# Output projection by block products: where the weights' parts are made, and which queues and engines carry the residual and the results

## The chip, the core and the metric

The kernel runs on one core of one Trainium2 chip. The core has five engines that run side by side, each with its own queue of instructions: TensorE (PE, matrix products into PSUM banks), VectorE (DVE), ScalarE (ACT), GpSimd (POOL) and SyncE (SP, which here only issues transfers). ACT and POOL can issue transfers too. The metric is the device time of one execution in microseconds, the median of several runs, smaller is better.

## The reference

One decoder block on x of shape (1, 2048, 1024), all in float32:

```python
h = rmsnorm(x, attn_norm);  z = h @ w_in          # pool | q | k | v | two gates
a = pool_mixer(...);        b = swa_sink_attention(...)
x = x + (g_pool * a + g_attn * b) @ w_out         # the output projection, w_out 1024 x 1024
h = rmsnorm(x, ffn_norm)
up = causal_depthwise_conv(h @ w_up, conv_w, conv_b)
x = x + (silu(up[..., :2816]) * up[..., 2816:]) @ w_down
```

The change concerns the third line, in the second half of the sequence.

## The kernel before, in words

**Chunks.** The 2048 positions are worked in two chunks of 1024 (`c` = 0, 1). In a chunk follow: keys and values (8 blocks), the attention loop (4 groups of 8 blocks, with projections as "fillers" between), the gates (`gates`, six units in chunk 1), the output projection, the up-projection (22 units) and the down-projection (`Down`).

**Three products for one.** A float32 operand is split into a high part (a cast by ACT) and the rest (a subtraction by DVE); a product is the sum of three matmuls of these parts. A split therefore costs one ACT and one DVE instruction per tile, and the result takes twice the room.

**Block products.** In chunk 1 the output projection uses Strassen's scheme in Winograd's form: w_out and its input are cut into 2 x 2 blocks, and seven products of sums of blocks replace eight. `PRODUCTS` (L198) lists them in order: A11·B11, A12·B21, S2·T2, S3·T3, A22·T4, S1·T1, S4·B22, called products 0 to 6 here. The A's and S's are blocks, or sums and differences of blocks, of w_out; the B's and T's are those of the input, made by `right_first`, `right_t1` to `right_t4` and `right_b22` (a subtraction on DVE and `parted`, a split). A product is 48 matmuls of 128x128 by 128x512 into four PSUM banks (`mul`), 8 steps of 6. The lists of banks `x` and `y` are shared: products 0, 2, 3 and 4 add into `x` one after the other, products 1, 5 and 6 use `y`, so a bank must be read out between two of them.

**Weights.** `out_factors` (L396) is a generator that the mixer of chunk 1 steps along, block by block in the keys' loop and in the attention loop. For each of four pairs of rows of blocks it loads `w_out` twice 512 KB into R tiles, and makes all seven A's and S's with 16 sums and differences in all. Each of the 28 results is split at once (`part`: ACT L406, DVE L407) into another R tile and stored to memory (`wo_A..`, `wo_S..`), both parts. `Out.weights` (L1242) later loads the two ready 1 MB tiles of one product, one product ahead of its use. R is a pool of three tiles (4 KB per partition), shared with the raw weights of the gates and of the up-projection; U is a pool of 19 tiles (8 KB).

**Results.** After product 0 `kept(0, 0)` (L1270) copies four banks, halved, by ACT (L1274) and adds the residual x by two transfers of POOL that accumulate into the tile (L1277); the same happens after products 2 and 3 for the other blocks. `final` (L1283) adds a finished bank to such a tile on DVE (L1285), squares it on ACT (L1289, L1292), adds up the squares for the next norm (DVE L1296), and stores the tile to `x2d` through SP. `residual` loads x plainly by SP instead. `stats` (L1346) sums the squares over channels by small matmuls (L669), takes the power on POOL (L662), and `whole` spreads the result by transposes (L680); `right_first` for the up-projection (L1177, then `parted`) needs that.

**Order.** The function `out_blocks` (L1303) is the text's order. On each engine the build lays out the instructions in one fixed order: text order is a preference, and an instruction whose inputs are expected ready can be put ahead. On the chip each engine then runs strictly in that order, so an instruction that waits holds up everything behind it on its engine. SP issues transfers in such an order too.

Of the kernel before, what the change touches and what calls it, by code (L numbers as in the profile page):

```python
# [26 lines left out]
P = 128  # L27
# [195 lines left out]
def block_kernel(ctx: ExitStack, tc: tile.TileContext, x, xT, pos, vec, qkn, w_poolT, w_pool, w_q, w_kv,  # L223
# [170 lines left out]
    out_parts = {name: dp.tile([P, 4, 2, 4, P], F32, f"wo_{name}") for name, _ in PRODUCTS}  # L394

    def out_factors():  # L396

        one, two = slice(4, 8), slice(0, 4)
        for i in range(4):
            g, v = (rp.tile([P, 8, P], F32, "R") for _ in range(2))  # L400
            load(g, w_out[i])
            load(v, w_out[i + 4])

            def part(name, src, i=i):
                t = rp.tile([P, 2, 4, P], F32R, "R")
                A.copy(t[:, 0], src)  # L406
                V.tensor_sub(t[:, 1], src, t[:, 0].bitcast(F32))  # L407
                load(out_parts[name][:, i], t.bitcast(F32))

            yield  # L410
            part("A11", g[:, one])
            yield
            part("A12", g[:, two])
            yield
            part("A22", v[:, two])
            yield
            V.tensor_sub(v[:, one], g[:, one], v[:, one])
            V.tensor_sub(v[:, two], v[:, two], v[:, one])
            part("S3", v[:, one])
            yield  # L420
            part("S2", v[:, two])
            yield
            V.tensor_add(g[:, one], g[:, one], v[:, two])
            part("S1", g[:, one])
            yield
            V.tensor_sub(g[:, two], g[:, two], v[:, two])
            part("S4", g[:, two])
            yield
# [801 lines left out]
    class Out:  # L1230


        def __init__(self, c):
            self.c, self.m, self.w, self.b, self.xs = c, [], [], {}, {}
            self.accs = [[], []]
# [16 lines left out]
        def mul(self, i, banks, first=False, by_pair=False):  # L1252

            w, r = self.w[i], self.b[PRODUCTS[i][1]]
            for n in range(8):
                j, m = divmod(n, 4) if by_pair else divmod(n, 2)[::-1]
                at = 0
                for k in range(2):
                    for a, b in ((0, 0), (0, 1), (1, 0)):
                        nc.tensor.matmul(banks[m], w[m // 2][:, m % 2, a, (2 * j + k + 2) % 4],  # L1260
                                         r[j][:, b, k], start=(first and j == 0 and at == 0),
                                         stop=(j == 1 and at == 5), skip_group_check=True)
                        at += 1
                yield n
# [5 lines left out]
        def kept(self, h, n, banks):  # L1270

            x = self.xs[h, n] = up_.tile([P, 4, 512], F32, "U")
            for m in range(4):
                A.activation(x[:, m], banks[m], AF.Copy, scale=0.5)  # L1274
            for i in range(2):
                m = slice(2 * i, 2 * i + 2)
                G.dma_start(x[:, m], self.rest(h, n)[:, m], accum_op=ALU.add)  # L1277

# [4 lines left out]
        def final(self, h, n, m, bank):  # L1283
            x = self.xs[h, n][:, m]
            V.scalar_tensor_tensor(x, bank, 0.5, x, op0=ALU.mult, op1=ALU.add)  # L1285
# [11 lines left out]
            load(x2d[4 * h + m][:, n * 512:n * 512 + 512], x)  # L1297
# [5 lines left out]
    def out_blocks(ob):  # L1303
# [19 lines left out]
        run(1, y, True, True)  # L1323
        t2s = right_t2(ob.m, ob.b, None)
# [3 lines left out]
        run(2, x)  # L1328
        right_t3(ob.m, ob.b)
        ob.kept(0, 1, x)  # L1330
        ob.weights()
        run(3, x)
        right_t4(ob.m, ob.b, t2s)
        ob.residual(1, 0)
        ob.kept(1, 1, x)
        ob.weights()
        for n in ob.mul(4, x):
            if n % 2 == 1:
                ob.final(1, 0, n // 2, x[n // 2])
        right_b22(ob.m, ob.b)  # L1340
        ob.weights()
        stream.fetch(stream.used + 1)
        stream.part(stream.used + 1)
# [8 lines left out]
        for n in ob.mul(5, y, True):  # L1352
            if n == 2:
                stats(0)
# [7 lines left out]
        for n in ob.mul(6, y):  # L1362
            if n == 0:
                for j in range(2, 4):
                    right_first(xg, b, j, pb)
# [4 lines left out]
            if n % 2 == 1:  # L1370
                ob.final(0, 1, n // 2, y[n // 2])
# [238 lines left out]
    def gates(c, units, b, xg, last_probabilities, last_values, last_filler):  # L1610


        def weights(f, n):
            if f < len(units):
# [6 lines left out]
                if n and w.at == 4:  # L1621
                    stream.fetch(stream.used + (1 if c > 0 or f + 1 < len(units) else 2))
# [49 lines left out]
        for f in range(2, n):  # L1672
# [9 lines left out]
            if f == n - 1 and c > 0:  # L1682
# [3 lines left out]
                ob.weights()  # L1686
            elif f == n - 1:
                mixes = {j: mixed(j) for j in (3, 2, 1)}
# [386 lines left out]
```

## Time and profile before

| | us |
|---|---|
| Median of 3 runs (2422.41 to 2429.26) | 2424.63 |
| The profiled execution | 2422.86 |
| Its span, first to last instruction | 2421.1 |
| TensorE busy in the span | 2370.1 |
| VectorE busy | 1907.9 |
| ScalarE busy | 1181.4 |
| GpSimd busy | 186.5 |

All breakdowns come from the profiled execution; between its span and its time lie 1.8 us. A row of the timeline gives start and length in us, engine, line, operation, output and input tiles, shape and count, and in brackets how long the engine had been idle and what released it. A row of a group by line gives busy us, mean ns of one, and the idle time ahead of the group with its releasers. "s", "a", "t" and "f" are PSUM tiles. `<-issue` means that the profile shows no other engine or transfer that was waited for. The granted clock is TensorE's, 1.00 at full speed.

### The profile page before, as it was taken

Reading aid. Unit: us, or ns where it says so; the run is one execution under the profiler, and the core shown is the slowest. Engines: PE = TensorE matmul, PEld = TensorE weight load, DVE = VectorE, ACT = ScalarE, POOL = GpSimd, SP = SyncE. Lnnn points to the kernel's source line nnn. Section 1 sums busy time; section 2 is a strip of 40 time slices with the busy share of each in tenths; the row PEclk is TensorE's granted clock in tenths of the full one; section 3 lists DMA queues with packets and bytes.
Section 4 is the critical chain, followed back from the end, with each engine's and each line's share of the span. In section 5 each row is a group of like instructions: output and inputs, shape, how many; then the busy total and the mean of one; then the engine's idle time right before and its main releaser. Section 6 shows DMA issues by size and latency. Waiting matters only on the chain.

```text
span 2421.1 us, 30322 instructions
## 1 busy us (share of the span) xinstructions
PE 2370.1 (98%) x11080; PEld 1962.8 (81%) x11080; DVE 1907.9 (79%) x2948; ACT 1181.4 (49%) x2166; POOL 186.5 (8%) x128
## 2 busy tenths in 40 slices
PE   8999998999999999999999999999999999999999
PEld 8888887877888888788888788778778888888887
DVE  8687887876977777899956878787478777779994
ACT  7455455454555555643533554454336545454432
POOL 1123111000000000000002232200100000000000
PEclk9999999999999999999999999999999999999999
DMA  9767777688222333644354797766842222228411
GB/s 342 245 202 234 226 227 260 211 290 293 80 79 91 101 105 105 213 167 142 125 214 139 231 296 240 234 205 248 286 161 90 90 90 79 79 70 287 139 70 53
DMA packets 167349, 425.94 MB, mean 176 GB/s; under 512 B 14624, under 2 KB 50976, under 8 KB 155680
## 3 DMA queue, kind: packets, MB, share of 16 engines
q1 hardware_dynamic: 160784, 412.28, 49.7%
q0 software_dynamic: 5984, 11.54, 3.0%
q8 instruction: 87, 1.43, 0.2%
q14 instruction: 62, 0.51, 0.1%
q10 hardware_dynamic: 432, 0.19, 0.0%
HBM read 274.66 MB, written 149.29 MB: 175 GB/s over the span
## 4 chain that ended last, share of the span: by engine, by line
PE 47%; DVE 4%; DMA 3%; issue 3%; ACT 1%; POOL 0%; SPq 0%; POOLq 0%; DVEq 0%; ACTq 0%
PE f L1225 11%; PE t L1225 6%; PE f L266 5%; PE f L1846 4%; PE a L1846 4%; PE s L1846 4%; PE t L1846 4%; PE a L1225 3%; PE a L266 1%; DMA U<-xT 1%; DVE F L1030 1%; PE a L974 1%; PE s L1260 1%; DMA tad<-U 1%; PE s L913 1%
## 5 line engine op out<-in xcount | busy, mean ns | idle before, releaser
L266 PE MATMUL f<-U,U 128*128 128x512 f32 (+1 forms) x2496 | 586.6, 390 | 9.6 <-ACT U L249 4.8
L266 PEld LDWEIGHTS f<-U,U 128*128 128x128 f32 x2496 | 457.2, 188 | 105.2 <-DVE U L250 7.3
L1225 PE MATMUL f<-U,U 128*128 128x512 f32 x1872 | 448.1, 390 | 6.9 <-ACT Q L1387 3.4
L1225 PEld LDWEIGHTS f<-U,U 128*128 128x128 f32 x1872 | 351.1, 188 | 83.5 <-ACT Q L1387 5.5
L1435 DVE SCALAR_TENSOR_TENSOR M<-F,vc,M 128x1024 f32<-128x1024 f32 x176 | 225.1, 1281 | 140.8 <-ACT M L1432 140.5
L1225 PE MATMUL t<-U,U 128*128 128x512 f32 x1332 | 316.1, 390 | 0.2 <-ACT Q L1387 0.2
L1225 PEld LDWEIGHTS t<-U,U 128*128 128x128 f32 x1332 | 250.5, 188 | 52.7 <-ACT Q L1387 0.8
L362 ACT CAST U<-R 128x1024 fp32r<-128x1024 f32 x147 | 153.7, 1053 | 87.3 <-DVE R L391 42.8
L1225 PE MATMUL a<-U,U 128*128 128x512 f32 x756 | 184.6, 391 | 0.0
L363 DVE TENSOR_TENSOR U<-R,U 128x1024 fp32r<-128x1024 f32 x147 | 179.2, 1221 | 3.0 <-ACT U L362 3.0
L1225 PEld LDWEIGHTS a<-U,U 128*128 128x128 f32 x756 | 141.3, 188 | 29.3 <-ACT Q L1387 0.2
L1225 PE MATMUL f<-U,M 128*128 128x512 f32 x624 | 151.1, 390 | 0.8 <-DVE F L1413 0.8
L932 ACT ACTIVATE Q<-s,st,rq 128x128 f32<-128x128 f32 x256 | 113.9, 455 | 68.7 <-DVE st L929 65.7
L1225 PEld LDWEIGHTS f<-U,M 128*128 128x128 f32 x624 | 116.9, 188 | 26.1 <-DVE F L1413 1.9
L954 POOL TENSOR_SCALAR_AFFINE_SELECT M<-M 128x1024 fp32r<-128x1024 f32 x64 | 96.8, 1512 | 387.7 <-DVE st L934 270.4
L1421 ACT COPY F<-f 128x512 f32<-128x512 f32 x52 | 30.6, 588 | 185.7 <-PE f L1225 185.7
L1804 ACT CAST U<-U 128x1024 fp32r<-128x1024 f32 x76 | 79.0, 1051 | 82.9 <-PE a L1846 24.4
L1432 ACT ACTIVATE M<-F,vc 128x1024 f32<-128x1024 f32 x88 | 109.4, 1243 | 2.0 <-DVE F L1417 0.5
L1805 DVE TENSOR_TENSOR U<-U,U 128x1024 fp32r<-128x1024 f32 x76 | 91.9, 1218 | 2.9 <-ACT U L1804 2.7
L1804 ACT CAST F<-U 128x1024 fp32r<-128x1024 f32 x44 | 46.2, 1050 | 90.9 <-PE a L1846 61.3
L1387 ACT COPY Q<-f 128x512 f32<-128x512 f32 x104 | 60.9, 585 | 52.8 <-PE f L1225 52.8
L981 ACT COPY U<-a 128x512 f32<-128x512 f32 x64 | 37.5, 586 | 95.4 <-PE a L974 95.0
(308 smaller groups left out, 3915.6 us busy)
## 6 DMA issues: line engine op xcount, KB each, us to landing
R<-w_up SPq DMA_DIRECT2D x80, 512.0 KB, 3.7
actd<-M SPq DMA_DIRECT2D x44, 512.0 KB, 2.6
U<-w_down SPq DMA_DIRECT2D x88, 256.0 KB, 4.8
U<-actd SPq DMA_DIRECT2D x88, 256.0 KB, 5.0
qd<-U SPq DMA_DIRECT2D x64, 256.0 KB, 3.8
Q<-qd SPq DMA_DIRECT2D x64, 256.0 KB, 5.0
R<-w_out SPq DMA_DIRECT2D x24, 512.0 KB, 5.7
U<-kept_S SPq DMA_DIRECT2D x12, 1024.0 KB, 6.9
```

Of the source, the lines that this page charges most:

```text
L266: nc.tensor.matmul(out, a, b, start=(i == 0), stop=(i == n - 1))
L362: A.copy(t[:, 0], raw)
L363: V.tensor_sub(t[:, 1], raw, t[:, 0].bitcast(F32))
L932: A.activation(pr[:, h, :], sc[:, h, 0:P], AF.Exp, bias=nm[:, h:h + 1], scale=it["rq"][:, h:h + 1], accum_out=rs[:, h:h + 1])
L954: G.affine_select(own.rearrange("p a h q -> p (a h) q"), pa.bitcast(F32).rearrange("p a h q -> p (a h) q"), pattern=[[0, 8], [1, P]], base ...
L1225: nc.tensor.matmul(bank, a[:, x, k, :], b[k // 2][:, y, k % 2, :], start=(first and i == 0), stop=(i == 11), skip_group_check=True)
L1387: Up.last = A.copy(t, bank).ins
L1432: A.activation(y, u[:, 2:], AF.Identity, bias=cw[:, 3, m:m + 1], scale=cw[:, 2, m:m + 1])
L1435: V.scalar_tensor_tensor(y, u[:, j:j + T], cw[:, j, m:m + 1], y, op0=ALU.mult, op1=ALU.add)
L1804: A.copy(hi, src)
L1805: V.tensor_sub(lo, src, hi.bitcast(F32))
L1846: nc.tensor.matmul(into[m], u[:, 0, c_], v[:, 1], start=(first and j == 0), stop=(k == n - 1 and j == 2), skip_group_check=True)
```

## The change

Four things, all in chunk 1:

1. `out_factors` no longer splits. It makes the sums and differences in place and stores two tiles of 512 KB per step (`wo_g`, `wo_v`); A11, A12 and A22 are read from `w_out` itself. `weights` loads the raw halves of one product (two 512 KB tiles, runs of 2 KB) into R tiles, and a new `split` makes the parts by ACT and DVE inside the output projection.
2. The residual of block (0, 0) is loaded plainly ahead of product 0, and `added` adds the banks to it on DVE. `kept` takes one bank at a time and is called inside the matmul loops.
3. `final` stores to `x2d` by ACT's queue.
4. The calls are put in another order, each product's split, T parts and next load right behind the first step of the product before; `right_first` for blocks 2 and 3 of the up-projection comes behind the last finals; the first raw weights of the up-projection are no longer fetched in the gates but in product 5.

```diff
     def out_factors():
         for i in range(4):
             g, v = (rp.tile([P, 8, P], F32, "R") for _ in range(2))
             load(g, w_out[i])
             load(v, w_out[i + 4])
-            def part(name, src, i=i):
-                t = rp.tile([P, 2, 4, P], F32R, "R")
-                A.copy(t[:, 0], src)
-                V.tensor_sub(t[:, 1], src, t[:, 0].bitcast(F32))
-                load(out_parts[name][:, i], t.bitcast(F32))
...
             yield
+            V.tensor_sub(v[:, F_], g[:, F_], v[:, F_])
+            V.tensor_sub(v[:, L_], v[:, L_], v[:, F_])
             yield
+            V.tensor_add(g[:, F_], g[:, F_], v[:, L_])
+            load(out_sums["v"][i], v)
+            V.tensor_sub(g[:, L_], g[:, L_], v[:, L_])
+            load(out_sums["g"][i], g)
             yield
...
         def weights(self):
-            name = PRODUCTS[len(self.w)][0]
-            ts = [up_.tile([P, 2, 2, 4, P], F32R, "U") for _ in range(2)]
-            for i, t in enumerate(ts):
-                load(t.bitcast(F32), out_parts[name][:, 2 * i:2 * i + 2])
+            src, at, half = OUT_W[PRODUCTS[len(self.raws)][0]]
+            raws = [rp.tile([P, 2, 4, P], F32, "R") for _ in range(2)]
+            for i, t in enumerate(raws):
+                load(t, src[at + 2 * i:at + 2 * i + 2, :, half].rearrange("m p k c -> p m k c"))
+            self.raws.append(raws)
+
+        def split(self):
+            ts = []
+            for raw in self.raws[len(self.w)]:
+                t = up_.tile([P, 2, 2, 4, P], F32R, "U")
+                A.copy(t[:, 0], raw)
+                V.tensor_sub(t[:, 1], raw, t[:, 0].bitcast(F32))
+                ts.append(t)
             self.w.append(ts)
...
-        def kept(self, h, n, banks):
-            x = self.xs[h, n] = up_.tile([P, 4, 512], F32, "U")
-            for m in range(4):
-                A.activation(x[:, m], banks[m], AF.Copy, scale=0.5)
-            for i in range(2):
-                m = slice(2 * i, 2 * i + 2)
+        def kept(self, h, n, m, bank):
+            if m == 0:
+                self.xs[h, n] = up_.tile([P, 4, 512], F32, "U")
+            x = self.xs[h, n]
+            A.activation(x[:, m], bank, AF.Copy, scale=0.5)
+            if m % 2 == 1:
+                m = slice(m - 1, m + 1)
                 G.dma_start(x[:, m], self.rest(h, n)[:, m], accum_op=ALU.add)
+
+        def added(self, h, n, m, bank):
+            x = self.xs[h, n][:, m]
+            V.scalar_tensor_tensor(x, bank, 0.5, x, op0=ALU.mult, op1=ALU.add)
...
-            load(x2d[4 * h + m][:, n * 512:n * 512 + 512], x)
+            A.dma_start(x2d[4 * h + m][:, n * 512:n * 512 + 512], x)
...
         ob.mix()
+        ob.residual(0, 0)
         run(0, x, True, True)
+        ob.split()
         ob.first(2)
         right_t1(ob.m, ob.b, None)
         ob.mix()
-        ob.kept(0, 0, x)
+        for m in range(4):
+            ob.added(0, 0, m, x[m])
         ob.weights()
         ob.first(3)
         run(1, y, True, True)
+        ob.split()
         t2s = right_t2(ob.m, ob.b, None)
         ob.weights()
         for m in range(4):
             ob.final(0, 0, m, y[m])
-        run(2, x)
-        right_t3(ob.m, ob.b)
-        ob.kept(0, 1, x)
-        ob.weights()
+        for n in ob.mul(2, x):
+            if n == 0:
+                ob.split()
+                right_t3(ob.m, ob.b)
+                ob.weights()
+            if n % 2 == 1:
+                ob.kept(0, 1, n // 2, x[n // 2])
...
         for n in ob.mul(5, y, True):
+            if n == 0:
+                ob.split()
+                stream.fetch(stream.used + 1)
+                stream.part(stream.used + 1)
...
         for n in ob.mul(6, y):
-            if n == 0:
-                for j in range(2, 4):
-                    right_first(xg, b, j, pb)
+            if n % 2 == 1:
+                ob.final(0, 1, n // 2, y[n // 2])
             if n == 3:
                 for f in range(2):
                     heads[f].fetch("A11", "A12")
                 stream.ahead().step(1)
-            if n % 2 == 1:
-                ob.final(0, 1, n // 2, y[n // 2])
+        for j in range(2, 4):
+            right_first(xg, b, j, pb)
...
-                if n and w.at == 4:
-                    stream.fetch(stream.used + (1 if c > 0 or f + 1 < len(units) else 2))
+                if n and w.at == 4 and (c == 0 or f + 1 < len(units)):
+                    stream.fetch(stream.used + (1 if f + 1 < len(units) else 2))
...
                 ob.weights()
+                ob.split()
```

Products 3 and 4 are treated as product 2 is. The matmul's weight index changes with the layout of the parts; its 48 matmuls per product stay.

More of the change, by code (lines that the diff above doesn't have):

```diff
@@ L392, in fourth @@
             self.halved("S1", "S4", g)
-    out_parts = {name: dp.tile([P, 4, 2, 4, P], F32, f"wo_{name}") for name, _ in PRODUCTS}
+    out_sums = {name: dp.tile([4, P, 8, P], F32, f"wo_{name}") for name in "gv"}
+    F_, L_ = slice(4, 8), slice(0, 4)
+    OUT_W = {"A11": (w_out, 0, F_), "A12": (w_out, 0, L_), "A22": (w_out, 4, L_),
+             "S3": (out_sums["v"], 0, F_), "S2": (out_sums["v"], 0, L_),
+             "S1": (out_sums["g"], 0, F_), "S4": (out_sums["g"], 0, L_)}
     def out_factors():
-        one, two = slice(4, 8), slice(0, 4)
         for i in range(4):
@@ L1327, in out_blocks @@
             ob.final(0, 0, m, y[m])
-        run(2, x)
-        right_t3(ob.m, ob.b)
-        ob.kept(0, 1, x)
-        ob.weights()
[L1332 to L1336, printed above, removed]
+        for n in ob.mul(2, x):
[5 more added lines that the diff above has]
+                ob.kept(0, 1, n // 2, x[n // 2])
+        for n in ob.mul(3, x):
+            if n == 0:
+                ob.split()
+                right_t4(ob.m, ob.b, t2s)
+                ob.weights()
+                ob.residual(1, 0)
+            if n % 2 == 1:
+                ob.kept(1, 1, n // 2, x[n // 2])
         for n in ob.mul(4, x):
+            if n == 0:
+                ob.split()
+                ob.weights()
+                right_b22(ob.m, ob.b)
             if n % 2 == 1:
                 ob.final(1, 0, n // 2, x[n // 2])
[L1340 to L1343, printed above, removed]
         norms, b = [], {}
```

26 lines of the change are left out of this document (7 added, 19 removed).

## The prediction

> **What bounds the kernel now.** I read the page's first part, then busy time by stretches, then TensorE's timeline for every place where it stood idle, then the engine that released it.
>
> ```profile
> span 2421.1 us, 30322 instructions
> ...
> PE 2370.1 (98%) x11080; PEld 1962.8 (81%) x11080; DVE 1907.9 (79%) x2948; ACT 1181.4 (49%) x2166; POOL 186.5 (8%) x128
> ```
>
> TensorE (PE) is busy for 98% of the span and the change removes no matmul, so a gain can only come from the 51 us (2421.1 − 2370.1) in which PE is idle, or from matmuls that run at a lower clock. The question is which of those lie where the change works: chunk 1's attention loop (the weight pieces made there), the output projection (1689 to 1776 us), and the head of the up-projection behind it. The busy times by stretches (start:end, length, then busy us of each engine):
>
> ```profile
> 1320.00:1511.00 191.00, 186.11 (x957) 155.49 (x956) 159.36 (x317) 98.44 (x307) 52.68 (x30) 1.00 0.78 247
> 1511.00:1560.00 49.00, 43.56 (x228) 36.04 (x227) 35.64 (x67) 22.05 (x63) 9.33 (x6) 1.00 0.71 224
> ...
> 1689.00:1776.00 87.00, 82.38 (x360) 67.36 (x359) 48.23 (x59) 32.18 (x46) 8.40 (x7) 0.96 0.77 247
> 1776.00:1812.00 36.00, 31.15 (x137) 24.52 (x138) 28.92 (x35) 15.18 (x22) 1.01 (x1) 0.95 0.54 190
> ```
>
> Idle PE: 4.9, 5.4, 4.6 and 4.9 us, and in the last two the granted clock is below 1. PE's timeline there (start, length; in brackets the idle time before and who ended it):
>
> ```profile
> 1725.82 8.63 PE L1260 MATMUL s<-U,U 128*128 128x512 f32 x24 [3.71 <-ACT U L1274]
> 1734.28 2.88 PE L1260 MATMUL a<-U,U 128*128 128x512 f32 x12
> ...
> 1775.87 2.99 PE L1225 MATMUL f<-U,U 128*128 128x512 f32 x12 [0.91 <-issue]
> 1780.65 0.35 PE L669 MATMUL a<-one,F 128*128 128x1 f32 x2 [1.79 <-DVE F L1296]
> ...
> 1784.51 0.66 PE L680 MATMUL s<-identr,M 128*128 128x128 f32 x2 [0.55 <-DVE M L678]
> 1784.82 3.84 PE L1225 MATMUL f<-U,U 128*128 128x512 f32 x12
> ...
> 1793.28 5.60 PE L1225 MATMUL a<-U,U 128*128 128x512 f32 x24
> ...
> 1807.79 1.43 PE L1225 MATMUL f<-U,U 128*128 128x512 f32 x5 [1.82 <-DVE U L1084]
> 1809.89 3.03 PE L1225 MATMUL f<-U,U 128*128 128x512 f32 x12 [0.68 <-ACT Q L1387]
> ```
>
> An idle time here costs twice: after the 3.71 us the 24 matmuls took 8.63 us, where 24 take 5.60 at 1793. The slices of 1 us show why (PE busy, then granted clock):
>
> ```profile
> 1730.00:1731.00 1.00, 1.00 (x4) 0.50 1.05 403
> ...
> 1785.00:1786.00 1.00, 1.00 (x4) 0.50 1.21 410
> ```
>
> So the first place costs 3.71 + 3.03 = 6.7 us. The second, behind the last product, costs 0.91 + 1.79 + 0.55 + (3.84 − 2.88) = 4.2 us, the third 1.82 + 0.68 = 2.5 us.
>
> **The 6.7 us.** Product 3 (S3) adds into banks that `kept(0, 1)` must read first (ACT L1274). ACT stood in front of that at another instruction, back to a POOL transfer:
>
> ```profile
> 1712.12 0.69 DVE L1285 SCALAR_TENSOR_TENSOR U<-f,U 128x512 f32<-128x512 f32 x1 [4.93 <-DMA U<-xT]
> ...
> 1721.10 0.69 DVE L1285 SCALAR_TENSOR_TENSOR U<-t,U 128x512 f32<-128x512 f32 x1 [6.56 <-DMA U<-xT]
> ```
>
> ```profile
> 1721.83 0.63 ACT L1292 ACTIVATE M<-U 128x512 f32<-128x512 f32 x1 [6.62 <-DVE U L1285]
> ```
>
> ```profile
> 1699.16 1.23 POOL L1277 DMA_DIRECT2D U<-xT  x1 [101.63 <-PE a L1260]
> 1712.35 1.22 POOL L1277 DMA_DIRECT2D U<-xT  x1 [11.95 <-issue]
> 1726.18 1.22 POOL L1277 DMA_DIRECT2D U<-xT  x1 [12.62 <-ACT U L1274]
> ```
>
> `kept(0, 0)` adds the residual by two accumulating DMAs from POOL. The second is issued 13.2 us after the first, when the first's data is there (1712.1 by DVE's row), so `final(0, 0)` gets its upper half at 1721.1. ACT's square waits behind it for 6.62 us, and `kept(0, 1)` behind that. The change loads this residual ahead by a plain load and adds it on DVE (`added`): no POOL transfer stands there any more, and the finals can run when product 1 ends. **Minus 6.7 us.** The four accumulates that are left start about 1717; at 13.2 us apart, the worst of these rows, the last is issued by 1757 and lands 8.8 us later (1712.35 to 1721.10), at 1766, where product 6 wants its bank free at about 1762. Bound 0 to +4; taken at 0, because 13.2 is an upper end.
>
> **What the parts cost.**
>
> ```profile
> L407 DVE TENSOR_TENSOR R<-R,R 128x512 fp32r<-128x512 f32 x28 | 22.2, 794 | 10.1 <-ACT R L406 9.8
> L406 ACT CAST R<-R 128x512 fp32r<-128x512 f32 x28 | 17.4, 622 | 25.7 <-DMA wo_A<-R 19.0 <-DMA wo_S<-R 3.0 <-DMA R<-w_out 2.0
> ```
>
> ```profile
> L1084 DVE TENSOR_TENSOR U<-U,U 128x1024 fp32r<-128x1024 f32 x13 | 15.5, 1218 | 9.9 <-ACT U L1083 9.9
> L1083 ACT CAST U<-U 128x1024 fp32r<-128x1024 f32 x14 | 14.3, 1049 | 6.0 <-DVE U L1177 5.1 <-DMA U<-xd 0.9
> ...
> L1285 DVE SCALAR_TENSOR_TENSOR U<-f,U 128x512 f32<-128x512 f32 x6 | 4.0, 686 | 10.7 <-DMA U<-xT 10.1 <-PE f L1260 0.6
> L1274 ACT ACTIVATE U<-s 128x512 f32<-128x512 f32 x6 | 3.2, 592 | 7.4 <-PE s L1260 7.4
> ```
>
> Out of the attention loop go 28 casts (17.4 us of ACT) and 28 subtractions (22.2 us of DVE); the 16 sums and differences of weights stay. Into the output projection come 14 splits of double width: 14 × 1.05 = 14.7 us of ACT and 14 × 1.22 = 17.1 us of DVE, by the rows of the same shape in `parted`. `added` puts 4 × 0.69 = 2.8 us on DVE and takes 4 × 0.59 = 2.4 us off ACT.
>
> *Attention.* What the loop's R buffers do to PE is seen at its end:
>
> ```profile
> 1517.31 0.69 DVE L382 TENSOR_TENSOR R<-R,R 128x512 f32<-128x512 f32 x1 [3.42 <-DMA R<-w_gp]
> ```
>
> ```profile
> 1519.08 0.46 ACT L932 ACTIVATE Q<-s,st,rq 128x128 f32<-128x128 f32 x1 [3.81 <-DVE st L929]
> ```
>
> ```profile
> 1521.00 1.22 PE L913 MATMUL s<-U,Q 128*128 128x256 f32 x8 [0.94 <-ACT Q L932]
> ...
> 1524.01 0.63 PE L946 MATMUL t<-identr,Q 128*128 128x128 f32 x4 [0.86 <-DVE Q L938]
> ```
>
> A gate weight came late because its R buffer was the last part's; DVE stood 3.42 us at it with the softmax queued behind, and PE lost 0.94 + 0.86. In the new loop the R tiles are free long before: **minus 1.8.** Of the 4.9 us idle in 1320 to 1511, with DVE at 159 of 191 us, I take a quarter, **minus 1.2** (bounds 0 and 4.9: nothing says how much hangs on the casts).
>
> *Output projection.* DVE and ACT hold 48 and 32 us of 87; with twelve of the splits (two fall ahead of 1689) they come to about 66 and 43, so neither is the bound as a sum. By product it is tighter:
>
> ```profile
> 1689.30:1700.20 10.90, 10.90 (x50) 9.02 (x49) 9.92 (x11) 6.63 (x9) 1.04 (x1) 1.00 0.57 210
> 1700.20:1711.10 10.90, 10.90 (x50) 9.03 (x49) 6.59 (x6) 3.55 (x4) 0.19 (x1) 1.00 1.04 356
> 1711.10:1722.00 10.90, 10.90 (x49) 8.79 (x47) 3.32 (x5) 2.38 (x4) 1.22 (x1) 1.00 0.67 189
> ```
>
> DVE's third column sums to 19.8 us for products 0 to 2. Due by their end are also the splits of products 1 to 3 (6 × 1.22 = 7.3), `added` (2.8), the rest of `final(0, 0)` that now slips past 1722 (four instructions, about 2.7), and T3's two parts (2.4): 35.0 us in 32.7. So DVE is over by **2.3 us**, and PE waits that long at product 2 or 3. Below it is 0, if T4's subtractions, done early now, move back; above it 8, if the wait falls on two products and one draws the half clock (2.3 + 2.3 + 3.0). I take 2.3: products 4 to 6 have room.
>
> *End of the stage.* B21's parts are traced behind the finals now, so `stats(1)` no longer queues behind them on DVE. B11's parts precede product 6, and u0's first product covers the statistics. I count 1.79 + 0.55 + 0.96 = **minus 3.3** (0.91 has no releaser, so I leave it), and in the up-projection's head, where the same chain hands T3 to PE, **minus 1.8**, leaving 0.68.
>
> *Transfers.* Weights: 28 stores become 8, and 14 loads of 1 MB become 14 of 512 KB.
>
> ```profile
> R<-w_up SPq DMA_DIRECT2D x80, 512.0 KB, 3.7
> ...
> U<-wo_S SPq DMA_DIRECT2D x8, 1024.0 KB, 12.3
> ```
>
> Three R buffers serve two tiles in 10.9 us, so a tile may be held 16.3 us, of which 1.05 + 1.22 for the split: a load may take 14 us. Both rows are below that; cost 0. The w_up pair, no longer fetched in the gates, gets R after product 6's split, about 30 us ahead of its first use.
>
> *Stores by ACT.* 16 issues at 0.39 us make 6.2 us of ACT, each behind the square of the same tile, so ACT waits for nothing new; casts for the next product queue behind them, with ACT then at about 49 of the stage's 87 us. SP loses its waits:
>
> ```profile
> 1.29 0.39 ACTq L468 DMA_DIRECT2D vc<-vec  x1
> ```
>
> ```profile
> SPq L243 <- DVE U L1285: 29.8, 14, 7.0
> ```
>
> No PE wait above ends in a load held up by them, so I count 0. The Trainium skill (DMA: Bandwidth & Descriptors, "Issuing engines are not separate DMA queues") says that issuing from a second engine saves only the sequencer's issue time. The row shows more than that to save, the 29.8 us of standing at the head of the queue; the sum is 0 by both.
>
> **Sum.** −6.7 − 1.2 − 1.8 + 2.3 − 3.3 − 1.8 = −12.5 us. The profiled execution took 2422.86 us (1.8 around its span), the median of the runs is 2424.63: 2410.4 on the one, 2412.1 on the other. I forecast **2412**. The Trainium skill (TensorE: Matmul & The Clock Gate, "What's actually happening") puts the return to half clock after at least one idle window of about 3.4 us. This trace has it at 1785 behind idle times of at most 1.79 us, so row and page differ; by the page the 0.96 would not belong to the idle time and the sum would be −11.5.
>
> **Rivals** (on the median's scale).
> 1. *The wait is replaced.* DVE's debt of products 0 to 2 reaches 7.6 us instead of 2.3, and it is carried on, so that the end of the stage and the up head keep their 3.3 and 1.8 us: −12.5 + 5.3 + 5.1 = −2.1, 2422. For it: DVE is over by my own count, and its subtractions waited 9.9 us for casts already. Against: 5 us of room per product from product 4 on. Chance 0.23.
> 2. *The order isn't the text's.* Engines run in an order that the build lays out, so `stats(1)` may stay behind other DVE work: −12.5 + 5.1 = −7.4, 2417, on the edge of a gain. Chance 0.14.
> 3. *Slower: loads late.* If a load of 512 KB in runs of 2 KB takes more than 14 us, the R ring limits the products. At 18 us a tile is held 20.3 us, a product gets its pair every 13.5 us, 2.6 late; six products make 16 us, and three half-clock spells 9. With the 2.3 gone: −14.8 + 25 = +10, 2435. For it: the stretch's transfers are crowded, 1.04 of 16 engines in product 1. Against: bytes per product halve. Chance 0.08.
>
> **Numbers.** My case has 0.55. About 0.3% (7.3 us) is what a measurement can tell. Faster: 0.55 and half of rival 2 make 0.62; same: rival 1 and the other half, 0.30; slower 0.08. The range runs from all idle time of the four places gone (6.7 + 4.2 + 2.5 + 1.8 + 4.9 = 20.1, 2404) to rival 1 with the accumulates' 4 us, 2426.
>
> **What would show it.** In the changed profile PE should have no idle time over 1 us between 1700 and 1735 and clock 1.00 there; POOL four accumulates; no DVE wait for U<-xT before product 4; the wait for R<-w_gp and its two PE gaps gone; at the stage's end the statistics' matmuls right behind u0's first product. I am wrong if PE waits for a subtraction of the new split (rival 1), or a split's cast for R<-wo (rival 3), or if idle time around the statistics stays (rival 2).

## The result and the profile after

The kernel after takes **2406.89 us** (median of 4 runs, 2405.84 to 2409.00); the kernel before, run beside it, 2426.1 us (4 runs, 2422.41 to 2429.26). The ratio is 0.9922 with a 95% interval of 0.9905 to 0.9940: 19 us less. The two profiled executions are 17.0 us of span apart (2421.1 and 2404.1), and those 17.0 us are what the traces can place.

Lines moved by the diff: a product's matmul is L1255 now (L1260 before), the up-projection's L1211 (L1225), the parts' subtraction L1070 (L1084); the new split is L1239 on ACT and L1240 on DVE.

The page of the kernel after, the same two lines as before:

```profile
span 2404.1 us, 30227 instructions
...
PE 2367.5 (98%) x11080; PEld 1963.3 (82%) x11080; DVE 1911.4 (80%) x2938; ACT 1177.1 (49%) x2148; POOL 182.8 (8%) x126
```

PE is busy 2.6 us less and idle 14.4 us less (36.6 instead of 51.0). The shorter busy time is that of the seven products (81.95 us before, 78.89 after), where the half clock behind the old gap is gone. To see where the idle time went, four moments that exist in both kernels serve as milestones: the first matmul of chunk 0's Down stage, of product 0, of the up-projection, and of chunk 1's Down stage. PE's timeline of before (the third, 1775.87, stands in the prediction), then of after:

```profile
1019.32 0.84 PE L1846 MATMUL f<-U 128*128 128x512 f32 x3
...
1689.30 2.88 PE L1260 MATMUL s<-U,U 128*128 128x512 f32 x12
...
2204.68 0.84 PE L1846 MATMUL f<-U 128*128 128x512 f32 x3
```

```profile
1018.45 0.84 PE L1860 MATMUL f<-U 128*128 128x512 f32 x3
...
1680.17 2.88 PE L1255 MATMUL s<-U,U 128*128 128x512 f32 x12
...
1728.37 3.06 PE L1255 MATMUL s<-U,U 128*128 128x512 f32 x12 [0.78 <-DVE U L1277]
...
1759.84 2.88 PE L1211 MATMUL f<-U,U 128*128 128x512 f32 x12
1762.56 0.28 PE L655 MATMUL a<-one,F 128*128 128x1 f32 x2
...
1787.70 1.43 PE L1211 MATMUL f<-U,U 128*128 128x512 f32 x5 [1.82 <-DVE U L1070]
1789.81 5.49 PE L1211 MATMUL f<-U,U 128*128 128x512 f32 x12 [0.68 <-ACT Q L1400]
1795.09 3.34 PE L1211 MATMUL t<-U,U 128*128 128x512 f32 x12
...
2187.29 0.84 PE L1860 MATMUL f<-U 128*128 128x512 f32 x3
```

| stretch | before | after | change | forecast |
|---|---|---|---|---|
| to chunk 0's Down stage (no changed code) | 1019.3 | 1018.5 | −0.9 | 0 |
| A: from there to product 0 (holds the attention loop) | 670.0 | 661.7 | −8.3 | −3.0 |
| B: products 0 to 6 | 86.6 | 79.7 | −6.9 | −4.4 |
| C: up-projection to chunk 1's Down stage | 428.8 | 427.5 | −1.4 | −5.1 |

(The forecast for B is the −6.7 and the +2.3; that for C is the end of the stage, whose waits lie behind the up-projection's first matmul, and the up head, which means the head of the up-projection. u0 is its first unit.) B's −6.9 is the 6.7 us, plus the 0.91 us ahead of u0's first matmul, which the forecast had left out, less a new wait of 0.78 us inside product 4. The statistics' matmuls (L655) stand right behind u0's first product. In the up head the 1.82 and 0.68 us are all there, and now the two groups of 12 matmuls behind them take 5.49 and 3.34 us instead of 2.88 each. The busy times by stretches, for the two attention stretches of before, the projection and the up head, and a slice of 1 us in that head:

```profile
1320.00:1511.00 191.00, 188.19 (x981) 158.63 (x980) 147.78 (x294) 87.96 (x289) 51.63 (x30) 1.00 0.68 204
1511.00:1560.00 49.00, 47.82 (x244) 40.28 (x243) 39.63 (x73) 25.31 (x74) 11.36 (x8) 1.00 0.69 209
...
1680.00:1760.00 80.00, 79.22 (x359) 65.38 (x358) 63.23 (x77) 38.46 (x52) 5.92 (x5) 1.00 0.74 231
1760.00:1800.00 40.00, 37.50 (x161) 30.18 (x160) 34.88 (x41) 16.09 (x22) 1.01 (x1) 0.91 0.25 87
1790.00:1791.00 1.00, 1.00 (x3) 0.81 (x4) 1.00 (x1) 1.00 (x2) 0.00 (x0) 0.50 0.00 0
```

DVE lost 11.6 us in the first stretch (159.36 to 147.78), ACT 10.5, and PE's idle time there fell from 4.9 to 2.8 us, in the next from 5.4 to 1.2. POOL's timeline has four accumulates:

```profile
1713.59 1.23 POOL L1273 DMA_DIRECT2D U<-xT  x1 [125.05 <-ACT U L1270]
1724.39 1.22 POOL L1273 DMA_DIRECT2D U<-xT  x1 [9.57 <-issue]
1730.76 1.22 POOL L1273 DMA_DIRECT2D U<-xT  x1 [5.16 <-issue]
1737.67 1.22 POOL L1273 DMA_DIRECT2D U<-xT  x1 [5.69 <-ACT M L1292]
```

### The profile page after: what moved, and what is told of

Same layout as the page of the kernel before. It is cut to its first block, busy times and chain, and to the rows that moved or that the text cites. A ratio compares the mean times of both kernels' runs of the same rounds, so it can differ in the third digit from the quotient of the medians.

```text
span 2404.1 us, 30227 instructions
## 1 busy us (share of the span) xinstructions
PE 2367.5 (98%) x11080; PEld 1963.3 (82%) x11080; DVE 1911.4 (80%) x2938; ACT 1177.1 (49%) x2148; POOL 182.8 (8%) x126
## 4 chain that ended last, share of the span: by engine, by line
PE 75%; DVE 3%; DMA 2%; ACT 1%; issue 1%; POOL 0%; SPq 0%; DVEq 0%; POOLq 0%; ACTq 0%
PE f L1211 23%; PE t L1211 12%; PE f L266 10%; PE a L1211 6%; PE f L1860 4%; PE a L1860 4%; PE s L1860 4%; PE t L1860 4%; PE a L266 1%; PE a L960 1%; PE s L899 1%; PE s L1255 1%; PE f L1255 1%; PE t L1255 1%; PE a L1255 1%
## 5 line engine op out<-in xcount | busy, mean ns | idle before, releaser
L1211 PE MATMUL f<-U,U 128*128 128x512 f32 x1872 | 451.1, 393 | 6.0 <-ACT Q L1400 3.4
L1211 PEld LDWEIGHTS f<-U,U 128*128 128x128 f32 x1872 | 353.2, 189 | 83.3 <-ACT Q L1400 5.5
L1211 PE MATMUL t<-U,U 128*128 128x512 f32 x1332 | 316.0, 390 | 0.0
L1211 PEld LDWEIGHTS t<-U,U 128*128 128x128 f32 x1332 | 250.7, 188 | 52.4 <-ACT Q L1400 0.2
L1211 PE MATMUL a<-U,U 128*128 128x512 f32 x756 | 183.9, 390 | 0.0
L1211 PEld LDWEIGHTS a<-U,U 128*128 128x128 f32 x756 | 141.3, 188 | 29.4 <-ACT Q L1400 0.2
L1211 PE MATMUL f<-U,M 128*128 128x512 f32 x624 | 150.8, 390 | 0.7 <-DVE F L1426 0.7
L1211 PEld LDWEIGHTS f<-U,M 128*128 128x128 f32 x624 | 116.9, 188 | 26.0 <-DVE F L1426 1.8
L1818 ACT CAST U<-U 128x1024 fp32r<-128x1024 f32 x76 | 79.1, 1050 | 84.5 <-PE a L1860 25.6
```

What stands on the lines that cost most here:

```text
L1211: nc.tensor.matmul(bank, a[:, x, k, :], b[k // 2][:, y, k % 2, :], start=(first and i == 0), stop=(i == 11), skip_group_check=True)
L1818: A.copy(hi, src)
```

## The experiments

Theory A was the prediction's own account with a larger share for the attention: the plain residual load closes the gap ahead of product 3, the new weights' path frees the attention, the order of B21's parts saves the statistics' wait, and the stores' queue is worth nothing. Each run below is set against a rival that its expectation names. The table has the time, the ratio to the kernel before on the same chip with its interval, and the stretches of the profiled execution by the milestones above. The runs come from more than one chip, so the ratios are what is compared, not the medians.

| run | median us | ratio | A | B | C |
|---|---|---|---|---|---|
| before (runs shown) | 2424.6 | 1 | 670.0 | 86.6 | 428.8 |
| after | 2406.9 | 0.9922 (0.9905–0.9940) | 661.7 | 79.7 | 427.5 |
| e1 residual only | 2419.3 | 0.9972 (0.9962–0.9981) | 669.2 | 80.3 | 430.3 |
| e2 weights only | 2416.8 | 0.9969 (0.9954–0.9983) | 662.9 | 85.6 | 427.3 |
| e3 stores by SP | 2414.2 | 0.9949 (0.9934–0.9964) | 663.1 | 84.3 | 427.4 |
| e4 end order as before | 2405.6 | 0.9917 (0.9903–0.9932) | 662.4 | 80.0 | 425.0 |
| e5 T3 behind T2 | 2407.6 | 0.9915 (0.9901–0.9930) | 663.6 | 79.4 | 426.3 |
| e6 loop work back | 2407.4 | 0.9920 (0.9904–0.9937) | 662.9 | 79.2 | 424.5 |
| e7 R held | 2404.8 | 0.9910 (0.9895–0.9924) | 660.6 | 79.3 | 426.2 |
| e9 w_up in the gates | 2426.8 | 1.0001 (0.9992–1.0010) | 662.4 | 99.7 | 427.4 |
| e10 part stores by ACT | 2434.2 | 1.0032 (1.0019–1.0044) | 676.4 | 85.0 | 429.2 |
| e11 third R tile | 2410.0 | 0.9934 (0.9916–0.9952) | 666.2 | 79.1 | 427.3 |
| e12 w_up behind T3 | 2411.4 | 0.9942 (0.9926–0.9959) | 661.1 | 79.6 | 430.7 |

How far can one profile's stretch be trusted? After, e2, e3, e4, e5, e9 and e12 run the same attention loop, and their A lies between 661.1 and 663.6; before and e1 share the old one, 670.0 and 669.2. So A is good to about 1.3 us either way. The stretch ahead of it, which no run changes, lies between 1017.8 and 1021.4, so one profile can be off by somewhat more.

**e1: the residual alone.** The kernel before, with `kept(0, 0)` replaced by a load ahead and four additions:

```diff
+        ob.residual(0, 0)
         run(0, x, True, True)
...
-        ob.kept(0, 0, x)
+        for m in range(4):
+            ob.added(0, 0, m, x[m])
```

> The kernel before with one edit: the residual of block (0, 0) is loaded ahead by SP and added on DVE, in place of POOL's two accumulating transfers. Theory A (the terms are separate): PE's 3.71 us gap ahead of product 3 and the half clock behind it go, product 0 still starts at about 1689 us, time minus 6 to 7 us against the kernel before. Rival B (the gap hangs on the whole order of finals and parts, so that another instruction ahead of kept(0, 1) on ACT takes the wait over): minus 0 to 2 us, and a gap of 2 us or more stays between products 2 and 3.

The ratio makes −6.8 us (interval −4.6 to −9.2), the stretch B −6.3, as Theory A has it. PE's timeline shows what is left of the idle time in the stage and behind it:

```profile
1709.61 2.56 PE L1260 MATMUL f<-U,U 128*128 128x512 f32 x10 [0.48 <-DVE U L1084]
...
1777.60 0.42 PE L680 MATMUL s<-identr,M 128*128 128x128 f32 x2 [0.86 <-DVE M L678]
```

The 3.71 us and the half clock behind it are gone. So are the 1.79 us at the statistics, though B21's parts stand where they stood before, so their place alone was not the cause. What follows at the spread of the statistics got worse: 0.86 us of waiting and 4.60 us for 12 matmuls, 2.6 us too much, where before had 0.55 + 0.96 = 1.5.

**e2: the weights alone.** The kernel before with the new loop, the loads and splits one product ahead and w_up fetched outside the gates; residual, stores and end order as before.

```diff
-            part(...) x28, each with a store
+            load(out_sums["v"][i], v); load(out_sums["g"][i], g)
...
         run(0, x, True, True)
+        ob.split()
```

> The kernel before with the weights' path alone changed: the loop makes and stores only sums, the parts are split one product ahead inside the output projection, the first raw weights of the up-projection are fetched in product 5; residual, finals and stores as before. Theory A: product 0 starts about 8 us earlier (1681), and the wait ahead of product 3 stays at 3.7 us and its half clock; time minus 8. Rival B: the attention loop owes its gain to other edits, product 0 starts less than 4 us earlier. Rival C (the prediction's debt of DVE): the output projection is longer than the 86.6 us of before by 3 us or more, because the splits stand among the parts and finals.

Stretch A falls by 7.1 us to within the scatter of the kernel after, B by 1.0: the gap ahead of product 3 shrinks, against the expectation, and a new one opens inside product 4 (PE's timeline). The profiled execution is one of the shortest of this run, 2411.6 us against a median of 2416.8.

```profile
1714.59 5.74 PE L1255 MATMUL s<-U,U 128*128 128x512 f32 x24 [1.16 <-ACT U L1269]
...
1734.09 4.62 PE L1255 MATMUL s<-U,U 128*128 128x512 f32 x12 [3.78 <-DVE U L1280]
```

The matmuls behind the 3.78 us are at half clock again (12 in 4.62 us). So Theory A's separate terms do not hold: e2 keeps the two accumulates of `kept(0, 0)`, but POOL issues them 6.6 us apart here, not 13.2 as before, and with them the gap ahead of product 3 shrinks. Between the two issues the DMA share is 0.82 here and was 1.04 before; that the other loads made the accumulates slow is likely, not shown. e2, too, has no wait at the statistics, and 0.88 us at their spread. By the ratios e1 has 6.8 us, e2 7.5, and e3 below, which has everything but the stores' queue, 12.4 of the 19; intervals of 2 to 4 us either way leave it open how far the first two overlap.

**e3: the stores back on SP.** One line of the kernel after:

```diff
-            A.dma_start(x2d[4 * h + m][:, n * 512:n * 512 + 512], x)
+            load(x2d[4 * h + m][:, n * 512:n * 512 + 512], x)
```

> The changed kernel with the x2d stores issued by SP again. Theory A: PE waits for no load that stands behind a store, time within 1.5 us of the changed kernel. Rival: SP stands at each store until DVE has the final, the raw weights of the next product are issued behind it, and PE waits for a split; plus 3 us or more, with idle time of PE before products 3 to 6 that ends in the split.

The stores' queue is worth 6.5 us by the ratios (0.9949 against 0.9922, with intervals that just overlap) and 4.6 us in stretch B, where Theory A had nothing. PE's timeline; SP's waits for finals (total us, times, longest) from 1680 to 1735, then from 1680 to 1770; and DVE's timeline ahead of the 2.62 us:

```profile
1715.02 3.02 PE L1255 MATMUL s<-U,U 128*128 128x512 f32 x12 [0.90 <-ACT U L1270]
...
1735.26 4.61 PE L1255 MATMUL s<-U,U 128*128 128x512 f32 x12 [2.62 <-DVE U L1277]
```

```profile
SPq L243 <- DVE U L1277: 3.2, 4, 2.5
```

```profile
SPq L243 <- DVE U L1277: 28.0, 15, 5.1
```

```profile
1733.38 1.23 DVE L1240 TENSOR_TENSOR U<-R,U 128x1024 fp32r<-128x1024 f32 x1 [2.72 <-ACT U L1239]
1734.52 0.68 DVE L1277 SCALAR_TENSOR_TENSOR U<-s,U 128x512 f32<-128x512 f32 x1
```

The chain reads backwards: inside product 4, PE may go on in tile `s`, which holds two of the banks, only when `final` (L1277) has read its first half; `final` stands on DVE behind a split (L1240, product 6's) that waited 2.72 us for its cast, and the cast had waited 2.90 us for its raw weights. SP issued that load 41.4 us after product 0's first matmul; in the kernel after it is 39.1 us. Ahead of it SP had stood 3.2 us at four stores; the other 24.9 of the 28.0 us lie behind it, where no product's weights are loaded any more. So 3.2 us of standing, not 28, came ahead of the load that was 2.3 us later. Some of DVE's and ACT's instructions also stand in another order in the two builds, so this last link is argued, not shown alone. In the kernel after, SP has no wait for L1277. The Trainium skill (DMA: Bandwidth & Descriptors, "Issuing engines are not separate DMA queues") says that issuing from several engines saves only the time that the sequencer needs to issue. This run bears that out only in part: the 16 issues take 0.33 us each on ACT (the median of L1297 in the kernel after), 5.2 us in the whole stage and 1.3 us for the four ahead of the late load, while the queue also stood at these four until DVE had computed their data.

**e4: the end's order as before.** The kernel after, with `right_first(xg, b, j, pb)` for j = 2, 3 ahead of the last finals again.

> The changed kernel with right_first of blocks 2 and 3 back ahead of the last finals in product 6. Theory A: PE's wait of 1.8 us for the last sum of squares and the 0.5 us for the spread come back with some half clock, while the wait in the up-projection's head (1.82 + 0.68 us and 3.1 us of half clock) may lose its half clock: plus 1 to plus 4 us. Rival: DVE's order is laid out by expected readiness, so the text's order does nothing: 0.

2405.6 us, within the interval of the kernel after, and no wait at the statistics or their spread. The reorder of `right_first` brought nothing, as the rival has it. Of what it was credited with, the 1.79 us are gone in e1 and e2 as well; the waits at the spread are gone in the kernel after, e3 and e4 but not in e1 or e2, and no run shows which edit removed them.

**e9: w_up fetched in the gates.** The kernel after, with the fetch condition of before, so that two of the three R tiles hold w_up while the products run:

```diff
-                if n and w.at == 4 and (c == 0 or f + 1 < len(units)):
-                    stream.fetch(stream.used + (1 if f + 1 < len(units) else 2))
+                if n and w.at == 4:
+                    stream.fetch(stream.used + (1 if c > 0 or f + 1 < len(units) else 2))
```

> The kernel after, with the w_up pair fetched in the gates again, as before: during the projection's products one R tile, not three, is left to the new weights. Theory A (three R tiles are enough and fewer are not): a product's two loads follow one another through one tile, a load and a split each, about 7 to 8 us a piece against 5.45 us of product; products 2 to 5 start 2 to 5 us late each and the half clock comes with the waits: the stage takes 90 us or more instead of 79.7, time 2417 or above. Rival (the ring was no limit and that part of the change was idle): the stage stays within 1.5 us of 79.7 and the time within 2 us of 2406.9.

The whole gain is gone (1.0001), B is 99.7 us. The stretch of the seven products, and ACT's group of the split's casts from 1675 to 1770:

```profile
1681.70:1781.40 99.70, 88.26 (x357) 70.73 (x356) 66.29 (x78) 42.11 (x56) 5.92 (x5) 0.91 0.57 173
```

```profile
L1239 ACT CAST U<-R 128x1024 fp32r<-128x1024 f32 x12 | 12.6, 1048 | 22.6 <-DMA R<-wo_v 9.0 <-DMA R<-wo_g 7.4 <-DMA R<-w_out 6.3
```

ACT stands 22.6 us at loads of raw weights, and everything in its queue with it: PE is idle 11.4 us and its clock 0.91. In the kernel after, the same row has 3.8 us. Three tiles are enough; one is not; two were not tried.

**e6 and e7: what in the attention loop cost time.** e7 is the kernel after with before's seven steps for each pair of rows, the added ones empty, so that R is held as long as before; e6 puts 28 casts' and 28 subtractions' worth of work into these steps, in place and without effect on the values:

```diff
+            def work(src):
+                A.copy(src, src)
+                V.tensor_max(src, src, src)
...
+            yield
+            work(g[:, F_])
```

> The kernel after, with before's seven steps for each pair of rows in the attention loop, and in them 28 in-place copies on ACT and 28 in-place maxima on DVE of the old parts' shapes, which change no value; no third R tile, no part stored. From chunk 0's Down stage to product 0 before took 670.0 us and after 661.7. Theory W (the attention gained because the 28 casts and subtractions left): 667 us or more, time about 2413. Theory S (it gained because the part tiles and their stores left the R ring): 664 us or less, time about 2408 or less. The projection's own stage (79.7 us) stays as after by both.

> The kernel after, with before's seven steps for each pair of rows in the attention loop and no work in the added ones: the R pair of w_out is held as long as before. Theory H (the hold of the R tiles alone delays the loads behind them): the stretch from chunk 0's Down stage to product 0 is 665 us or more instead of 661.7, time about 2411. Theories W and S: it stays within 1 us of 661.7, time within 1.5 us of 2406.9. What e6 has above this run is the price of the 28 casts and subtractions; what before has above e6 is that of the third R tile and its stores.

A is 662.9 and 660.6, both inside the scatter of the kernel after. Theory W, that the casts and subtractions themselves held PE up, is refuted, Theory H too.

**e11 and e10: the third tile and its stores.** e11 gives e7's steps before's cast and subtraction into a third R tile, without a store; e10 is the kernel before with the parts' stores issued by ACT:

```diff
+                t = rp.tile([P, 2, 4, P], F32R, "R")
+                A.copy(t[:, 0], src)
+                V.tensor_sub(t[:, 1], src, t[:, 0].bitcast(F32))
```

```diff
-                load(out_parts[name][:, i], t.bitcast(F32))
+                A.dma_start(out_parts[name][:, i], t.bitcast(F32))
```

> The kernel after, with before's seven steps for each pair of rows in the attention loop, and in each a third R tile with before's cast and subtraction written into it; none of these parts is stored. The run with the same work in place took 663.0 us from chunk 0's Down stage to product 0, before took 670.0. Theory Q (the stores in SP's queue): within 1.5 us of 663, time about 2407. Theory R (the third R tile): 667 us or more, time about 2413.

> The kernel before, with the 28 stores of the parts in the attention loop issued by ACT's queue instead of SP's; nothing else differs. Theory Q (in the attention SP stands at the head of its queue at these stores, 73 us by the profile of before, and the loads behind them come late): from chunk 0's Down stage to product 0 it takes 665 us or less instead of 670.0, and the time is about 2420. Theory R (the third R tile, taken until its store is done, delays the weights' loads and ACT's casts): it stays at 668 us or more, time 2423 to 2428. The projection's own stage stays as before, 86.6 us, by both.

e11's A is 666.2, between the two theories' bounds: 3.3 us above e6, 3.0 to 3.8 below before and e1. So the tile seems to cost about half of the stretch's loss and its stores the other half, with one profile each and 1.3 us of scatter; by total time e11 and e6 overlap (0.9934 and 0.9920). Of e11's 3.3 us over e6 only 1.2 are idle time of PE, the other 2.1 are longer matmuls, so this division is rough. e10 lost 7.8 us, against Theory Q in its plain form and beyond what Theory R expected: SP's wait for L407 fell from 59.1 to 7.8 us, but ACT's rows, from 1019 to 1570, show more waiting,

```profile
ACT R L406 <- DMA wo_A<-R: 29.0, 8, 5.4
ACT R L406 <- DMA wo_S<-R: 21.7, 8, 6.4
```

against 19.0 and 3.0 us in before. How the stores' half divides between SP's queue and the transfers themselves stays open.

**e5 and e12: the wait in the up head.** DVE makes T3's sums there ahead of a part of T2 that PE wants sooner. e5 orders them behind it (`tc.issue_after`), e12 also a step of w_up's weights.

> The kernel after, with the DVE work for T3 in chunk 1's up head ordered behind T2's last part, and T4's behind T3's; nothing else differs. Theory A (the 1.82 us wait of the up head is an order of DVE: T3's and T4's subtractions run ahead of the part of T2 that TensorE wants next): the wait of 1.82 us for U and the one of 0.68 us behind it go, and the half clock of 3.1 us with them, 2.5 to 5.6 us less than after, about 2402. Rival (DVE has as much to do in any order): T3 is then what comes late, by about the same, and the time stays within 1.5 us of after's 2406.9.

> The kernel after, with T3's and T4's DVE work ordered behind T2's and T3's parts as in the run before, and the first steps of w_up's weights of the third unit ordered behind T3's parts too: about 2 us of DVE work less ahead of TensorE's wait in chunk 1's up head. Theory A2 (DVE has more to do ahead of T2's last part than TensorE's 18.7 us of work cover): the 1.27 and 0.80 us of waits of that run shrink to less than 0.7 together, no half clock follows, time about 2402. Rival (what is pushed back becomes the next wait): waits of 1.5 us or more in the up head, time as after, 2405 to 2409.

PE's timeline of e5, then of e12:

```profile
1792.50 0.51 PE L1211 MATMUL f<-U,U 128*128 128x512 f32 x1 [1.27 <-ACT Q L1400]
1793.81 4.22 PE L1211 MATMUL f<-U,U 128*128 128x512 f32 x11 [0.80 <-DVE U L1070]
```

```profile
1766.42 0.35 PE L655 MATMUL a<-one,F 128*128 128x1 f32 x2 [2.48 <-DVE F L1296]
1767.65 0.38 PE L655 MATMUL a<-one,M 128*128 128x1 f32 x2 [0.88 <-ACT M L1292]
...
1794.87 0.50 PE L1211 MATMUL f<-U,U 128*128 128x512 f32 x1 [1.27 <-ACT Q L1400]
1795.64 4.38 PE L1211 MATMUL f<-U,U 128*128 128x512 f32 x11 [0.27 <-DVE U L1070]
```

2.50 us of waiting became 2.07 in e5, with the half clock behind it still there. In e12 it became 1.54, but 3.36 us opened at the statistics. DVE's timeline has the reason:

```profile
1751.69 0.69 DVE L1277 SCALAR_TENSOR_TENSOR U<-t,U 128x512 f32<-128x512 f32 x1 [5.16 <-DMA U<-xT]
```

The last accumulate, issued at 1740.19, was there 11.5 us later, and the finals behind it, with their sums of squares, came late; in the kernel after it took 8.8 us (1737.67 to 1746.49) and DVE waited 1.18. Whether the new order caused that is not shown. Neither run beats the kernel after; nor do e4, e6 and e7 outside their intervals.

## Why the prediction was right, and where its steps were not

- **−6.7, the gap ahead of product 3: right** in mechanism and size. e1 alone has −6.8, and in the kernel after the projection has clock 1.00 and 0.8 us of idle time. e2 adds that the accumulates' 13.2 us was no fixed price.
- **Accumulates at 0: right, with little to spare.** The last of the four is issued at 1737.67, ahead of product 5's end; they are 10.8, 6.4 and 6.9 us apart, where the bound had 13.2 for each. e12 has the loss that the bound allowed for: a last accumulate 2.7 us slower came with 3.4 us of waiting at the statistics.
- **The attention at −3.0: the mis-sized term.** It measured −8.3. The −1.8 at R<-w_gp came: both PE gaps are gone. The −1.2 for everything else was priced by the busy time of casts and subtractions, of which e6 shows that it costs nothing that can be told from the scatter. By e6 and e7 what is left, 670.0 − 662.9 = 7.1 us, goes with the third R tile and its stores. How they hold up PE isn't traced through: ACT's 22 us of waiting for stores, in the prediction's row of L406, is not the price as it stands, since in e6 ACT waits 21.9 us for R<-w_out at its copies (L407), and A stays within the scatter of the kernel after. The gaps themselves are to be read. PE's idle time in A is 12.4 us before, 5.9 after, 7.0 in e6, 8.3 in e11 and 17.8 in e10, and most of it stands at tiles of the softmax (Q by ACT and DVE), at more places than the one at R<-w_gp. PE's timeline of before has three more; in the kernel after these have 0.68, 0 and 1.18 us:

```profile
1479.46 1.22 PE L913 MATMUL s<-U,Q 128*128 128x256 f32 x8 [1.31 <-ACT Q L932]
...
1555.19 1.22 PE L913 MATMUL s<-U,Q 128*128 128x256 f32 x8 [1.70 <-ACT Q L932]
1559.29 0.63 PE L946 MATMUL t<-identr,Q 128*128 128x128 f32 x4 [1.94 <-DVE Q L938]
```

- **+2.3, DVE's debt: wrong.** No wait came by product 3. DVE by product, and its rows for the splits of products 1 and 3:

```profile
1680.20:1691.00 10.80, 10.80 (x49) 8.97 (x48) 10.80 (x14) 2.48 (x3) 0.00 (x0) 1.00 0.28 86
1691.00:1701.90 10.90, 10.90 (x49) 9.02 (x49) 9.55 (x10) 6.45 (x7) 0.00 (x0) 1.00 0.45 164
1701.90:1712.80 10.90, 10.90 (x49) 9.01 (x48) 10.90 (x13) 8.42 (x13) 0.00 (x0) 1.00 0.60 208
```

```profile
1672.59 1.22 DVE L1240 TENSOR_TENSOR U<-R,U 128x1024 fp32r<-128x1024 f32 x1
...
1674.92 1.22 DVE L1240 TENSOR_TENSOR U<-R,U 128x1024 fp32r<-128x1024 f32 x1
...
1703.10 1.21 DVE L1240 TENSOR_TENSOR U<-R,U 128x1024 fp32r<-128x1024 f32 x1
...
1704.84 1.21 DVE L1240 TENSOR_TENSOR U<-R,U 128x1024 fp32r<-128x1024 f32 x1
```

  DVE was nearly full (10.80, 9.55 and 10.90 us in three products), but not in debt. The step that failed is the count of what falls into products 0 to 2: it had the splits of products 1 to 3 there, and product 1's two, 2.4 us, ran ahead of product 0 (1680.17), which is the size of the debt. Product 3's are done at 1706.05, 6.8 us ahead of that product.
- **−3.3, the end of the stage: the waits went, the reason was wrong.** Rival 2 rightly doubted the order's worth: e4 has the old order and no wait, e1 loses the 1.79 us without the new one. What removed the 0.55 + 0.96 us at the spread stays open; e1 and e2 each still have more than that there.
- **−1.8 in the up head: wrong.** An earlier T3 was to shorten the wait, but PE waits there for T2's second part: in the kernel after DVE makes it at 1786.43, behind the sums of T3 and T4, in before at 1806.52, behind those of T3. The 1.82 us are the same in before, e1, e2, e3, e6 and e7, whenever the statistics are spread; that DVE's chain and PE's cover both start at that spread fits this, but is argued. The half clock that followed, (5.49 + 3.34) − 2 × 2.88 = 3.1 us, took back most of the end's 3.3. C's −1.4 has 1.2 us more than these two leave; e6, with 0.1 us in place of the 3.1, has a C 2.9 us shorter than the kernel after.
- **Transfers at 0: short by 0.78 us.** The prediction named a split's cast that waits for R<-wo as a sign of rival 3, and it is there: PE's 0.78 us inside product 4 go back to it. ACT's timeline in the kernel after, then DVE's:

```profile
1724.06 1.05 ACT L1239 CAST U<-R 128x1024 fp32r<-128x1024 f32 x1 [1.89 <-DMA R<-wo_g]
```

```profile
1725.15 2.56 DVE L1240 TENSOR_TENSOR U<-R,U 128x1024 fp32r<-128x1024 f32 x2 [2.22 <-ACT U L1239]
1727.63 0.68 DVE L1277 SCALAR_TENSOR_TENSOR U<-s,U 128x512 f32<-128x512 f32 x1
```

  e9 puts the price of too few tiles at 19 us. Rival 3's mechanism was real, and what keeps it small is the moved fetch of w_up. That fetch was not about 30 us ahead of its first use either: DVE stands 4.77 us at R<-w_up until 1733.08, which cost PE nothing there.
- **Stores by ACT at 0: wrong**, by 6.5 us by the ratios and 4.6 in B (e3). The prediction sought a wait that ended in a held load in the trace of before, where the products' weights had been split long ahead. With loads one product ahead even 3.2 us of standing came with a late load. It left the sum alone, because the forecast counted no loss by held loads in the first place.

In the profiled spans: −12.5 as forecast, −5.3 more in A, −2.5 more in B, +3.7 in C, and −0.5 in stretches without changed code make −17.0 (each rounded). The forecast lay 5 us above the measured median and within its wide range. That it lay so near is partly luck: the gain in A was nearly three times the term for it, a debt of 2.3 us did not come, and the half clock in the up head, also not forecast, took part of that back.

## What to carry to other kernels

The busy time of a group of instructions isn't the price of removing it: here 28 casts and subtractions cost nothing that could be measured, while the buffer and the stores that came with them cost about 7 us. When a change turns early loads into just-in-time loads, price again every store in the same in-order queue whose data is still being computed: waits that cost nothing before can become waits of the main engine. And count ring buffers by who holds them in the stretch: the same loop was 19 us better or no better at all by three tiles or one.

## What the runs showed of the hardware

Equal idle times are not followed by equal clocks. The waits of 1.82 and 0.68 us in the up head, five matmuls (1.4 us) between them, are the same in the kernel after, e6 and e7. PE's timeline of e6 and of e7 right behind them:

```profile
1793.25 3.01 PE L1227 MATMUL f<-U,U 128*128 128x512 f32 x12 [0.68 <-ACT Q L1416]
```

```profile
1789.37 4.61 PE L1216 MATMUL f<-U,U 128*128 128x512 f32 x12 [0.68 <-ACT Q L1405]
```

The extra time was 3.1 us in the kernel after, 1.7 in e7 and 0.1 in e6. The same two waits, to 0.01 us, stand in before, e1, e2, e3, e9, e10 and e11: 12 matmuls behind them took 4.90 to 5.49 us in e1, e3, e9 and e11, and 3.02 to 3.06 in before, e2 and e10. The Trainium skill (TensorE: Matmul & The Clock Gate, "What's actually happening") wants an idle window of about 3.4 us for the half clock; here 2.5 us in two pieces sufficed in six kernels and not in four. So the half clock behind a short wait is a chance to be priced between none and all, not a fixed surcharge. Each kernel has one profiled execution, so it is open whether the kernel or the execution decides; what decides it was not tried.
